# FoX bias masks behind the q and k normalisations, one weight piece loaded ahead of half of x, and x's norm begun a tick earlier

## The chip, the cores and the metric

The kernel runs on one core of one Trainium2 chip. The time is the device time of one execution in microseconds. Five engines take part: TensorE (PE, matmuls and transposes, with its weight loads listed apart as PEld), VectorE (DVE), ScalarE (ACT), GpSimd (POOL) and SyncE (SP), which issues most of the loads. Each engine works through its own instructions in the order in which they were written down. A row such as "PE ps_a L567 <- POOL raw L541" says that PE, at line 567, waited for POOL's work of line 541.

## What is computed

One decoder layer on 512 tokens of width 1024, in f32: three token mixers on the same normalised input, merged through gates, and a SwiGLU FFN. Cut to the parts that matter here:

```python
h = rms_norm(x, g_mix)
proj = h @ w_in
(q_m, k_m, v_m, q_f, k_f, v_f, f_logit, q_c, a_m, a_f, a_c) = jnp.split(proj, split_points, axis=-1)

# FoX: 8 heads of 64; cum is the running sum of the log forget gates
log_f = jax.nn.log_sigmoid(f_logit + b_forget).transpose(0, 2, 1)
q_f = rms_norm(split_heads(q_f, FOX_HEADS), g_q_fox)
k_f = rms_norm(split_heads(k_f, FOX_HEADS), g_k_fox)
scores = jnp.einsum('bhqd,bhkd->bhqk', qc, k) * scale + cq[..., None] - cum[:, :, None, :]
scores = jnp.where(causal, scores, -jnp.inf)
p = jax.nn.softmax(scores, axis=-1)

# cross attention into 256 memory tokens
mkv = rms_norm(mem, g_mem) @ w_mem_kv

merged = (sigmoid(a_m) * (y_m @ w_br_moba) + sigmoid(a_f) * (y_f @ w_br_fox)
          + sigmoid(a_c) * (y_c @ w_br_mem))
x = x + merged @ w_out
h2 = rms_norm(x, g_ffn)
x = x + (silu(h2 @ w_gate) * (h2 @ w_up)) @ w_down
```

## The kernel before

**Arithmetic.** Every f32 operand is split in two parts: ACT copies the rounded part (hi) and DVE subtracts it from the whole (lo). A product is three matmuls: hi by hi, hi by lo, lo by hi. Weights come in pieces of 128 x 1024 through SP (`load_next`, tile w_raw), and `split_next` turns each into w_hi (ACT, L223) and w_lo (DVE, L226).

**Order of the work.** All engines' orders come from one program that is written along PE's matmuls. `mm` (L291 issues the matmul) calls `tick` after each 1.25 us of matmuls by its own count, which here is every 6 matmuls of 512 columns. A tick issues at most one weight split, then what `later(n, fn)` has put off until n ticks on (`run_due`), then steps from the queue `side` (filled by `beside(steps, rate)`, so many steps a tick), and last the entries of `pend`. So a number n in `later(n, ...)` sets where an instruction stands in its engine's queue, not when it runs.

**The start.** SP loads mem in two halves, four pieces of w_mem_kv, the four tiles x0 to x3 of x (128 tokens each), then the other pieces. PE transposes mem (L436) and runs `mem_groups`, four pieces of w_mem_kv for the memory's keys, then four for its values. Beside that run the steps listed after `last_square`: squares and sums of x (`square_x`, ACT L618) and of mem (`mem_square`, ACT L451), `rsqrt` in three stages (variance: DVE L343; estimate: ACT L347 and L348; newton: DVE L351 to L353), the scaling of x (`scale_x`, L623: POOL for x0 and x1, DVE for x2 and x3), and `turn_x`, which transposes x on PE (L635). The evictions of the first memory group are ACT's raw (L519) and their squares sqh (L521).

**FoX.** The heads are done in two blocks, pairs 2 and 3 first, pairs 0 and 1 later. `head_chunk` projects q and k of a block into four quarters of raw, ACT evicts and squares them, `rsqrt` makes rr, and POOL normalises raw with rr, four instructions of 128x512 (`norm`, L541) put off by 5 to 8 ticks. With lag = 11, PE transposes the pairs 11, 13, 15 and 17 ticks on (`turn_pair`, L567), q and k in turn; ACT and DVE evict them to qT and kT (L579, L583). A tick after a k, `double` copies kT's halves across partitions, by DMAs that POOL issues (L587, L588). The forget bias of each head comes back from DRAM through ACT's queue (`load_bias`, tile ckb), and `mask_bias` writes a second copy of it with the causal mask added, one POOL instruction of 128x512 a head (L1144). `attention` runs in side steps: scores on PE (L893), bias and row minimum on DVE, exp on ACT, division on POOL (p_t, L926), transposes (L944) and values (L955) on PE. What PE does meanwhile are the gates (`gate_part`) and the branch projections (`branch_part`) of MoBA's branch.

Of the kernel before, what the change touches and what calls it, by code (L numbers as in the profile page):

```python
# [22 lines left out]
D = 1024  # L23
# [19 lines left out]
def hybrid_layer(ctx, tc, rope, x, mem, g_mix, w_in, b_forget, g_q_moba, g_k_moba, g_q_fox,  # L43
# [12 lines left out]
    def slot(name, dt=F32):  # L56
        return U.tile([P, SLOT], dt, name=name, tag="u", bufs=NSLOT)
# [3 lines left out]
    def use_table(name):  # L61
        if table[0] != name:
            act.preload_act_table_set(name)
            table[0] = name
# [16 lines left out]
    def sm(name, w, bufs=6):  # L81
        return small.tile([P, w], F32, name=name, tag=name, bufs=bufs)
# [87 lines left out]
    def load_next():  # L170
        i = loads[st["load"]]
        st["load"] += 1
        kind, src, nk, w = pieces[i]
        r = raws[i] = slot("w_raw")
        dst = r[:, :nk * w].rearrange("p (k c) -> p k c", k=nk)
        if kind == "wide":
            n = w // len(src)
            for c, part in enumerate(src):
                nc.sync.dma_start(dst[:, :, c * n:(c + 1) * n], part)
            return  # L180
        if kind == "add":
            nc.sync.dma_start(dst, src[0])
            for more in src[1:]:
                nc.gpsimd.dma_start(dst, more, accum_op=OP.add)
        else:
            nc.sync.dma_start(dst, src)
# [72 lines left out]
    pend = []  # L259
# [44 lines left out]
    def beside(steps, rate):  # L304
        side.extend((rate, fn) for fn in steps)

    def later(n, fn):
        deferred.append([n, fn])
# [18 lines left out]
    def rsqrt(ss, inv_n, w, delay=None, rows=None, nh=1, out=None):  # L327

        v, y0, a, r = (sm(i, 32, 6 if i == "rr" else 3) for i in ("rv", "ry", "ra", "rr"))
        v, y0, a = v[:, :w], y0[:, :w], a[:, :w]
        r = r[:, :w] if out is None else out

        def by_rows(o, i):
            o3, i3 = (q.rearrange("p (t h) -> p t h", h=nh) for q in (o, i))
            dve.tensor_tensor(o3, i3, rows[:, :, None].to_broadcast([P, w // nh, nh]), op=OP.mult)

        def variance():
            if rows is not None:  # L340
                by_rows(ss, ss)
                by_rows(ss, ss)
            dve.tensor_scalar(v, ss, inv_n, EPS, op0=OP.mult, op1=OP.add)  # L343

        def estimate():
            use_table("natural_log_exp_and_others")
            act.activation(a, v, AF.Ln)  # L347
            act.activation(y0, a, AF.Exp, scale=-0.5)  # L348

        def newton():  # L350
            dve.tensor_tensor(a, y0, y0, op=OP.mult)  # L351
            dve.scalar_tensor_tensor(a, a, -0.5, v, op0=OP.mult, op1=OP.mult)
            dve.scalar_tensor_tensor(r, a, 1.5, y0, op0=OP.add, op1=OP.mult)  # L353
            if rows is not None:
                by_rows(r, r)
        for n, stage in enumerate((variance, estimate, newton)):
            if delay is None:
                stage()
            else:
                later(delay + n, stage)  # L360
        return r
# [13 lines left out]
    def load_x():  # L375
        r = slot("x_t")
        t = len(x_t)
        nc.sync.dma_start(r[:, :D], x[0, t * P:(t + 1) * P, :])
        x_t.append(r)
# [11 lines left out]
    NG = 22  # L391
    GMIX, GFFN, GQF, GQM, GQC, GKF, GKM, GKC = 0, 8, 16, 17, 18, 19, 20, 21
    grow = consts.tile([NG, P], F32, name="grow")
    for _ in range(3):
        load_x()
    nc.gpsimd.dma_start(grow[0:8], g_mix.rearrange("o (k p) -> (o k) p", p=P))
    nc.gpsimd.dma_start(grow[8:16], g_ffn.rearrange("o (k p) -> (o k) p", p=P))
# [129 lines left out]
    def head_rest(raws, tw, ss, ntok, d, kind, blocks, lag, rows=None, e=2):  # L527
# [3 lines left out]
        if rows is not None:  # L531
            e = lag - 5
        rs = rsqrt(ss[:, :w], 1.0 / d, w, e, rows=rows, nh=nh)

        def of_tiles(t0, n):
# [73 lines left out]
    QF, KF_, VF = {}, {}, {}  # L609
# [5 lines left out]
    ssx = sm("ssx", NT, 1)  # L615

    def square_x(t):
        act.activation(slot("junk")[:, :D], x_t[t][:, :D], AF.Square, accum_out=ssx[:, t:t + 1])  # L618

    def scale_x(t):  # L620
        r = rsx[t // 2][:, t % 2:t % 2 + 1]
        e = pool if t < 2 else dve
        e.tensor_scalar(x_t[t][:, :D], x_t[t][:, :D], r, 1.0, op0=OP.mult, op1=OP.mult)  # L623

    rsx = {}

    def rms_x(half):
        rsx[half] = rsqrt(ssx[:, 2 * half:2 * half + 2], 1.0 / D, 2, 1)
        later(4, lambda: scale_x(2 * half))
        later(4, lambda: scale_x(2 * half + 1))  # L630

    def turn_x(k):
        tb = bank("a")
# [143 lines left out]
    def rms_mem():  # L777
        dve.tensor_reduce(ssm, ssp.rearrange("p (t a) -> p t a", a=2), axis=AX.X, op=OP.add)
        rsqrt(ssm, 1.0 / D, 2, 1, out=rs_mem)

    def both(f, *args):
        return lambda: [f(*a) for a in args]

    def last_square(t):
        square_x(t)
        rms_x(t // 2)

    beside([idle, idle, small_gains, lambda: square_x(0), lambda: last_square(1),
            lambda: square_x(2), lambda: last_square(3), both(mem_square, (0, 0), (1, 0)),
            both(mem_square, (0, 1), (1, 1)), rms_mem, idle]  # L790
           + [both(turn_x, (k,), (k + 1,)) for k in range(0, KD, 2)], 1.0)

    turn_mem(0, (split_next, split_next))
# [14 lines left out]
    YC, YM, YF = {}, {}, {}  # L808
# [275 lines left out]
    bias = {}  # L1084
# [57 lines left out]
    def mask_bias(h):  # L1142
        b = bias[h]
        pool.tensor_tensor(b[:, 512:1024].rearrange("p (a k) -> p a k", a=4),  # L1144
                           b[:, :512].rearrange("p (a k) -> p a k", a=4),
                           mz[:, None, 384:512].to_broadcast([P, 4, P]), op=OP.add)
# [4 lines left out]
    for h in (4, 5, 6, 7):  # L1151
        load_bias(h)
    for h in (4, 5, 6, 7):
        later(h, lambda h=h: mask_bias(h))
    later(17, lambda: beside(attention((2, 3), QF, KF_, VF, YF, bias), 0.7))
    for jc in (0, 1):
        gate_part(1, jc)
    for jc in (0, 1):
# [7 lines left out]
    v_chunk(VF, (0, 1))  # L1166
    for h in (0, 1, 2, 3):
        later(h + 1, lambda h=h: mask_bias(h))
    later(8, lambda: beside(attention((0, 1), QF, KF_, VF, YF, bias), 1.0))
    for jc in (2, 3):  # L1170
        gate_chunk(1, YM, jc)

# [451 lines left out]
    for p in range(NPAIR):  # L1624
# [5 lines left out]
        for m in ORDER:  # L1630
            n = at["d", m, p]
# [9 lines left out]
    for n, x in enumerate(order):  # L1641
# [3 lines left out]
        _, m, p = x  # L1645
# [49 lines left out]
```

## Time and profile before

| | us |
|---|---|
| median of 3 runs | 878.6 (877.55 to 878.94) |
| the profiled execution | 879.1 |
| its span, first to last instruction | 877.3 |
| PE busy | 849.8 (97%) |
| DVE busy | 658.1 (75%) |
| ACT busy | 471.4 (54%) |
| POOL busy | 223.1 (25%) |

The profiled execution's time is its span and 1.8 us around it. PE is busy almost throughout, and busy includes matmuls that run at the lower of the two granted clocks. A saving is therefore looked for where PE waits, and where its granted clock is below 1.

### The profile page before, as it was taken

What the parts mean: (1) busy time and instruction counts of PE and PEld (TensorE: products, weight loads), DVE (VectorE), ACT (ScalarE), POOL (GpSimd) and SP (SyncE); (2) the same over time, 40 slices, a digit from 0 to 9 for tenths busy, and PEclk for the clock granted to TensorE, in tenths of its full rate; (3) what the DMA queues carried; (4) which work ended last, traced back from release to release, by engine and by line L of the source; (5) the groups of instructions that cost most, each with busy time, mean ns of one, the idle gap of its engine ahead of it and who ended that gap; (6) DMA issues with size and microseconds to landing.
All of it is one profiled execution on the core that took longest, in us unless ns stands there. A gap on an engine that the chain in (4) does not pass through costs nothing.

```text
span 877.3 us, 13976 instructions
## 1 busy us (share of the span) xinstructions
PE 849.8 (97%) x5204; PEld 757.7 (86%) x5204; DVE 658.1 (75%) x1126; ACT 471.4 (54%) x816; POOL 223.1 (25%) x310
## 2 busy tenths in 40 slices
PE   7799999999999899999999999999999999999998
PEld 5588899799888678987888888999999999988886
DVE  4787699779677457658635845899888898997985
ACT  5855566567766546656632734544433344464671
POOL 4212218221522524244320003222311222110210
PEclk9899999999999999999999999999999999999999
DMA  9923248117521451423592536799986889775992
GB/s 310 336 30 88 57 119 216 27 49 195 129 64 41 129 121 49 121 73 85 155 240 78 172 87 144 159 193 193 179 165 124 168 169 192 174 187 146 238 249 98
DMA packets 141283, 126.10 MB, mean 144 GB/s; under 512 B 5840, under 2 KB 120072, under 8 KB 141216
## 3 DMA queue, kind: packets, MB, share of 16 engines
q1 hardware_dynamic: 107840, 95.21, 37.1%
q0 software_dynamic: 32192, 27.89, 20.8%
q10 hardware_dynamic: 1184, 2.12, 0.8%
q8 instruction: 41, 0.67, 0.3%
q14 instruction: 26, 0.21, 0.1%
HBM read 116.79 MB, written 4.21 MB: 138 GB/s over the span
## 4 chain that ended last, share of the span: by engine, by line
PE 75%; DVE 11%; ACT 6%; DMA 4%; issue 2%; POOL 2%; ACTq 0%; SPq 0%; DVEq 0%; POOLq 0%
PE ps_m L291 34%; PE ps_a L1365 12%; PE ps_m L1365 9%; PE ps_a L1518 9%; PE ps_m L1518 3%; PE ps_a L955 2%; DVE w_lo L226 2%; PE ps_a L893 2%; PE ps_a L944 2%; DMA w_raw<-in_w_mem_kv_dram 2%; ACT w_hi L223 1%; DMA kT<-kT 1%; DVE wl L1226 1%; POOL raw L541 1%; DMA mem_h<-in_mem_dram 1%
## 5 line engine op out<-in xcount | busy, mean ns | idle before, releaser
L226 DVE TENSOR_TENSOR w_lo<-w_raw,w_hi 128x1024 fp32r<-128x1024 f32 (+2 forms) x88 | 107.5, 1234 | 36.6 <-ACT w_hi L223 36.3
L291 PE MATMUL ps_m<-hT,w_hi 128*128 128x512 f32 x384 | 122.6, 401 | 0.0
L291 PE MATMUL ps_m<-w_hi,hT 128*128 128x256 f32 (+2 forms) x464 | 121.8, 337 | 0.0
L1365 PE MATMUL ps_a<-xh,wl 128*128 128x256 f32 x352 | 100.0, 284 | 1.0 <-DVE wl L1226 0.8
L1365 PE MATMUL ps_a<-xh,wh 128*128 128x256 f32 x352 | 99.8, 283 | 0.2 <-ACT wh L1223 0.2
L1365 PE MATMUL ps_a<-xl,wh 128*128 128x256 f32 x352 | 99.6, 283 | 0.0
L223 ACT ACTIVATE w_hi<-w_raw 128x1024 fp32r<-128x1024 f32 (+2 forms) x88 | 86.4, 1002 | 5.4 <-DMA w_raw<-in_w_mem_kv_dram 2.7
L291 PEld LDWEIGHTS ps_m<-w_hi,hT 128*128 128x128 f32 x464 | 80.1, 189 | 7.1
L291 PEld LDWEIGHTS ps_m<-hT,w_hi 128*128 128x128 f32 x384 | 70.9, 191 | 13.3
L1518 PE MATMUL ps_a<-dh,dr 128*128 128x512 f32 x242 | 76.6, 390 | 0.1
L291 PE MATMUL ps_m<-hT,w_lo 128*128 128x512 f32 x192 | 76.0, 396 | 0.0
L291 PE MATMUL ps_m<-w_lo,hT 128*128 128x256 f32 (+2 forms) x232 | 75.9, 327 | 0.0
L1365 PE MATMUL ps_m<-xh,wh 128*128 128x256 f32 x264 | 74.7, 283 | 0.0
L1365 PE MATMUL ps_m<-xl,wh 128*128 128x256 f32 x264 | 74.7, 283 | 0.0
L1365 PE MATMUL ps_m<-xh,wl 128*128 128x256 f32 x264 | 74.7, 283 | 0.0
L1200 POOL DMA_DIRECT2D wq<-in_w_gate_dram x22 | 32.0, 1456 | 151.7 <-DMA wq<-in_w_gate_dram 47.8
L1408 ACT ACTIVATE z<-z 128x512 f32<-128x512 f32 x22 | 13.9, 632 | 105.3 <-DVE z L741 105.3
L1365 PEld LDWEIGHTS ps_a<-xh,wl 128*128 128x128 f32 x352 | 67.5, 192 | 1.6 <-DVE wl L1226 1.6
L1226 DVE TENSOR_TENSOR wl<-wq,wh 128x1024 fp32r<-128x1024 f32 x55 | 66.9, 1218 | 2.1 <-ACT wh L1223 1.6
L1365 PEld LDWEIGHTS ps_a<-xh,wh 128*128 128x128 f32 x352 | 67.5, 192 | 0.4 <-ACT wh L1223 0.4
L1365 PEld LDWEIGHTS ps_a<-xl,wh 128*128 128x128 f32 x352 | 67.5, 192 | 0.0
L926 POOL TENSOR_SCALAR p_t<-p_t,rc 128x128 f32<-128x128 f32 (+1 forms) x64 | 36.1, 564 | 109.8 <-DVE rc L925 94.8
(271 smaller groups left out, 2212.8 us busy)
## 6 DMA issues: line engine op xcount, KB each, us to landing
w_raw<-in_w_in_dram SPq DMA_DIRECT2D x45, 512.0 KB, 4.7
wq<-in_w_gate_dram SPq DMA_DIRECT2D x55, 256.0 KB, 5.2
wq<-in_w_up_dram SPq DMA_DIRECT2D x55, 256.0 KB, 5.5
dq<-in_w_down_dram SPq DMA_DIRECT2D x25, 512.0 KB, 5.8
wq<-in_w_gate_dram POOLq DMA_DIRECT2D x22, 256.0 KB, 8.2
wq<-in_w_up_dram POOLq DMA_DIRECT2D x22, 256.0 KB, 10.4
dq<-in_w_down_dram POOLq DMA_DIRECT2D x10, 512.0 KB, 8.4
w_raw<-in_w_mem_kv_dram SPq DMA_DIRECT2D x8, 512.0 KB, 11.0
```

The source lines that it names most:

```text
L223: act.activation(hi[:, c], r[:, c], AF.Copy)
L226: dve.tensor_tensor(lo[:, c], r[:, c], f32(hi[:, c]), op=OP.subtract)
L291: pe.matmul(ps, lhsT, rhs, start=start, stop=stop)
L893: pe.matmul(ps[:, :n], Q[p][:, s * 512 + i * P:s * 512 + (i + 1) * P], K[p][s][:, b * 512:b * 512 + n], start=b == 0, stop=b == 1)
L926: pool.tensor_scalar(pt[:, :nk], pt[:, :nk], rc, 1.0, op0=OP.mult, op1=OP.mult)
L944: pe.transpose(tb[:, j * P:(j + 1) * P], pt[:, j * P:(j + 1) * P], ident)
L955: pe.matmul(yb[:, :256], V[p][:, j, 2 * s:2 * s + 2, :], PT[b][:, j, :], start=(j == 0 and b == 0), stop=(j == nj - 1 and b == 1))
L1200: e.dma_start(t[:, g * 512:(g + 1) * 512].rearrange("p (k c) -> p k c", k=4), dsrc(w, kh * 512 * DFF + f0 + fh * P, [[DFF, P], [P * DFF, 4 ...
L1226: dve.tensor_tensor(full(lo), full(r), f32(full(hi)), op=OP.subtract)
L1365: pe.matmul(ps[:, g * 256:(g + 1) * 256], w[a][:, g, k, :], r[b][:, k, :], start=n % 12 == 0, stop=n % 12 == 11)
L1408: act.activation(z[:, :, 0, :], z[:, :, 0, :], AF.Silu, scale=1.0 - 2 * j)
L1518: pe.matmul(acc_d[m][t2], r[a][:, e * 256 + t2 * P:e * 256 + (t2 + 1) * P], w[b][:, e * 512:(e + 1) * 512], start=(p == 0 and e == 0 and ( ...
```

## The change

There are three edits. In both FoX blocks the masks and the start of the attention are put off by more ticks. On SP, one more piece of weights is loaded between x1 and x2. At the start, x's squares 2 and 3 are put behind the squares of mem, and a `rsqrt` whose delay is 0 issues its variance at the end of the same tick.

```diff
         for n, stage in enumerate((variance, estimate, newton)):
             if delay is None:
                 stage()
+            elif delay + n == 0:
+                pend.append(stage)
             else:
                 later(delay + n, stage)
...
-    for _ in range(3):
+    load_x()
+    load_next()
+    for _ in range(2):
         load_x()
...
     def rms_x(half):
-        rsx[half] = rsqrt(ssx[:, 2 * half:2 * half + 2], 1.0 / D, 2, 1)
-        later(4, lambda: scale_x(2 * half))
-        later(4, lambda: scale_x(2 * half + 1))
+        rsx[half] = rsqrt(ssx[:, 2 * half:2 * half + 2], 1.0 / D, 2, 0)
+        later(2, lambda: scale_x(2 * half))
+        later(2, lambda: scale_x(2 * half + 1))
...
     beside([idle, idle, small_gains, lambda: square_x(0), lambda: last_square(1),
-            lambda: square_x(2), lambda: last_square(3), both(mem_square, (0, 0), (1, 0)),
-            both(mem_square, (0, 1), (1, 1)), rms_mem, idle]
+            both(mem_square, (0, 0), (1, 0)), both(mem_square, (0, 1), (1, 1)),
+            lambda: square_x(2), lambda: last_square(3), rms_mem, idle]
            + [both(turn_x, (k,), (k + 1,)) for k in range(0, KD, 2)], 1.0)
...
     for h in (4, 5, 6, 7):
-        later(h, lambda h=h: mask_bias(h))
-    later(17, lambda: beside(attention((2, 3), QF, KF_, VF, YF, bias), 0.7))
+        later(h + 5, lambda h=h: mask_bias(h))
+    later(19, lambda: beside(attention((2, 3), QF, KF_, VF, YF, bias), 0.7))
...
     for h in (0, 1, 2, 3):
         later(h + 1, lambda h=h: mask_bias(h))
-    later(8, lambda: beside(attention((0, 1), QF, KF_, VF, YF, bias), 1.0))
+    later(10, lambda: beside(attention((0, 1), QF, KF_, VF, YF, bias), 1.0))
```

POOL's queue at the first FoX block, before, from the first mask to the first copy of kT (ckb are the bias tiles of heads 4 to 7, raw the two tiles of q and k, rr the factor):

```order
L1144 TENSOR_TENSOR ckb_3317<-ckb_3317,mz_115 128x512
L541 TENSOR_TENSOR raw_2859<-raw_2859,rr_3316 128x512
L1144 TENSOR_TENSOR ckb_3319<-ckb_3319,mz_115 128x512
L541 TENSOR_TENSOR raw_2859<-raw_2859,rr_3316 128x512
L1144 TENSOR_TENSOR ckb_3321<-ckb_3321,mz_115 128x512
L541 TENSOR_TENSOR raw_2860<-raw_2860,rr_3316 128x512
L1144 TENSOR_TENSOR ckb_3323<-ckb_3323,mz_115 128x512
L541 TENSOR_TENSOR raw_2860<-raw_2860,rr_3316 128x512
L587 DMA kT_3480<-kT_3480 64x1024
```

The same place of POOL's queue in the changed kernel (line numbers from here on are higher by 4):

```order
L545 TENSOR_TENSOR raw_2859<-raw_2859,rr_3316 128x512 x2
L545 TENSOR_TENSOR raw_2860<-raw_2860,rr_3316 128x512 x2
L1148 TENSOR_TENSOR ckb_3317<-ckb_3317,mz_117 128x512
L1148 TENSOR_TENSOR ckb_3319<-ckb_3319,mz_117 128x512
L1148 TENSOR_TENSOR ckb_3321<-ckb_3321,mz_117 128x512
L1148 TENSOR_TENSOR ckb_3323<-ckb_3323,mz_117 128x512
L591 DMA kT_3480<-kT_3480 64x1024
```

The four normalisations now stand together ahead of the four masks; the copies of kT stay behind both.

PE's queue a little later, before, from the last transposes of this block (raw, of pair 3's k) to the first scores (kT by qT) between the matmuls of MoBA's branch projection (yT):

```order
L567 MATMUL ps_a<-ident,raw 128x128 x4
L291 MATMUL ps_m<-yT,w_hi 128x512 x2
L291 MATMUL ps_m<-yT,w_lo 128x512
L291 MATMUL ps_m<-yT,w_hi 128x512 x2
L291 MATMUL ps_m<-yT,w_lo 128x512
L893 MATMUL ps_a<-kT,qT 128x256 x2
```

And the same place of PE's queue in the changed kernel:

```order
L571 MATMUL ps_a<-ident,raw 128x128 x4
L291 MATMUL ps_m<-yT,w_hi 128x512 x2
L291 MATMUL ps_m<-yT,w_lo 128x512
L291 MATMUL ps_m<-yT,w_hi 128x512 x2
L291 MATMUL ps_m<-yT,w_lo 128x512
...
L291 MATMUL ps_m<-yT,w_hi 128x512 x2
L291 MATMUL ps_m<-yT,w_lo 128x512
L897 MATMUL ps_a<-kT,qT 128x256 x2
```

Instead of 6 matmuls, 18 stand between the last transposes and the first scores (of the 18, 9 repeat in the rows left out).

ACT's queue at the start, before, from the split of the fifth piece to that of the eighth (w_raw_154 is the fifth piece, x_t_96 and x_t_98 are x2 and x3, mem_h_74 the first half of mem, ps_m_160 and 161 the first memory group):

```order
L223 ACTIVATE w_hi_266<-w_raw_154 128x1024
L618 ACTIVATE junk_272,ssx_130<-x_t_96 128x1024
L223 ACTIVATE w_hi_281<-w_raw_200 128x1024
L347 ACTIVATE ra_258<-rv_256 128x2
L348 ACTIVATE ry_257<-ra_258 128x2
L618 ACTIVATE junk_288,ssx_130<-x_t_98 128x1024
L519 ACTIVATE raw_300<-ps_m_160 128x512
...
L223 ACTIVATE w_hi_318<-w_raw_214 128x1024
L451 ACTIVATE sqm_327,ssp_128<-mem_h_74 128x512 x2
L223 ACTIVATE w_hi_337<-w_raw_252 128x1024
```

The same stretch in the changed kernel, where w_raw_96 is the fifth piece and x_t_98 and x_t_100 are x2 and x3:

```order
L223 ACTIVATE w_hi_267<-w_raw_96 128x1024
L347 ACTIVATE ra_258<-rv_256 128x2
L348 ACTIVATE ry_257<-ra_258 128x2
L455 ACTIVATE sqm_274,ssp_130<-mem_h_74 128x512 x2
L223 ACTIVATE w_hi_284<-w_raw_200 128x1024
L455 ACTIVATE sqm_294,ssp_130<-mem_h_78 128x512 x2
L523 ACTIVATE raw_303<-ps_m_160 128x512
...
L223 ACTIVATE w_hi_321<-w_raw_214 128x1024
L622 ACTIVATE junk_326,ssx_132<-x_t_98 128x1024
L223 ACTIVATE w_hi_335<-w_raw_252 128x1024
L622 ACTIVATE junk_340,ssx_132<-x_t_100 128x1024
L223 ACTIVATE w_hi_354<-w_raw_270 128x1024
```

The squares of x2 and x3 stand behind those of mem and behind the two evictions raw (the rows left out are the first one's square sqh, the second raw and its square), one between each two of the following pieces. On DVE the Newton step of x2 and x3 now stands behind the low part of the ninth piece (w_raw_270).

## Rows read from the trace of the kernel before

**Rows 1.** What PE waited for: us in total, times, longest us.
```profile
PE ps_a L567 <- POOL raw L541: 3.8, 1, 3.8
...
PE ps_a L635 <- POOL x_t L623: 2.5, 2, 1.7
PE ps_a L635 <- DVE x_t L623: 2.0, 2, 1.8
PE ps_a L893 <- DMA kT<-kT: 1.8, 2, 1.1
...
PE ps_m L291 <- ACT raw L519: 1.2, 1, 1.2
...
PE ps_a L944 <- POOL p_t L926: 0.4, 1, 0.4
```

**Rows 2.** Timeline of PE, first FoX block: start, length, instruction, idle before.
```profile
301.26 0.49 PE L567 MATMUL ps_a<-ident,raw 128*128 128x128 f32 x3
305.52 0.48 PE L567 MATMUL ps_a<-ident,raw 128*128 128x128 f32 x1 [3.78 <-POOL raw L541]
305.65 1.20 PE L291 MATMUL ps_m<-hT,w_hi 128*128 128x512 f32 x2
...
311.33 0.70 PE L291 MATMUL ps_m<-hT,w_hi 128*128 128x512 f32 x2
...
314.52 0.71 PE L291 MATMUL ps_m<-hT,w_hi 128*128 128x512 f32 x2
...
320.06 0.47 PE L893 MATMUL ps_a<-kT,qT 128*128 128x256 f32 x2 [0.71 <-DMA kT<-kT]
```

**Rows 3.** Windows: length, busy time and instructions of each engine, granted clock, DMA.
```profile
305.60:310.90 5.30, 5.30 (x13) 4.05 (x14) 1.50 (x2) 1.36 (x2) 0.00 (x0) 0.50 0.01 3
...
36.40:41.30 4.90, 4.90 (x17) 4.22 (x18) 4.17 (x8) 1.90 (x5) 1.37 (x1) 0.50 1.07 325
```

**Rows 4.** Timeline of POOL, first FoX block.
```profile
295.73 1.04 POOL L541 TENSOR_TENSOR raw<-raw,rr 128x512 f32<-128x512 f32 x1 [3.54 <-DVE rr L353]
296.74 1.29 POOL L1144 TENSOR_TENSOR ckb<-ckb,mz 128x512 f32<-128x512 f32 x1
...
301.24 2.24 POOL L1144 TENSOR_TENSOR ckb<-ckb,mz 128x512 f32<-128x512 f32 x1
303.45 2.02 POOL L541 TENSOR_TENSOR raw<-raw,rr 128x512 f32<-128x512 f32 x1
314.25 0.57 POOL L587 DMA_DIRECT2D kT<-kT  x1 [8.78 <-DVE kT L583]
```

**Rows 5.** Timeline of DVE, first FoX block.
```profile
300.31 4.26 DVE L226 TENSOR_TENSOR w_lo<-w_raw,w_hi 128x1024 fp32r<-128x1024 f32 x2 [4.65 <-ACT w_hi L223]
```

**Rows 6.** The chain that ended last, at the first copy of kT.
```profile
314.25 5.68 DMA kT<-kT
```

**Rows 7.** Timeline of PE, second FoX block.
```profile
390.94 0.48 PE L893 MATMUL ps_a<-kT,qT 128*128 128x256 f32 x2 [1.14 <-DMA kT<-kT]
```

**Rows 8.** Timeline of ACT at the start.
```profile
17.54 1.06 ACT L618 ACTIVATE junk<-x_t 128x1024 f32<-128x1024 f32 x1 [0.57 <-DMA x_t<-in_x_dram]
...
21.43 1.06 ACT L223 ACTIVATE w_hi<-w_raw 128x1024 fp32r<-128x1024 f32 x1 [2.73 <-DMA w_raw<-in_w_mem_kv_dram]
...
25.75 0.57 ACT L519 ACTIVATE raw<-ps_m 128x512 f32<-128x512 f32 x1
...
28.04 1.04 ACT L223 ACTIVATE w_hi<-w_raw 128x1024 fp32r<-128x1024 f32 x1
28.99 0.61 ACT L451 ACTIVATE sqm<-mem_h 128x512 f32<-128x512 f32 x1
```

**Rows 9.** Timeline of DVE at the start.
```profile
33.60 0.16 DVE L353 SCALAR_TENSOR_TENSOR rr<-ra,ry 128x2 f32<-128x2 f32 x1
...
33.79 1.22 DVE L226 TENSOR_TENSOR w_lo<-w_raw,w_hi 128x1024 fp32r<-128x1024 f32 x1
34.93 1.41 DVE L623 TENSOR_SCALAR x_t<-x_t,rr 128x1024 f32<-128x1024 f32 x2
```

## The prediction

> **What bounds the kernel now.** I read the list of what TensorE (PE) waited for first, because PE is busy in nearly the whole span and only its waits and its slow clock can be won back. The list is short [rows 1]. Its longest entry is one wait of 3.8 us, at the transposes of FoX's normalised raw (L567) for GpSimd's L541. Two more entries are the transposes of x (L635), 2.5 and 2.0 us, at the start of the kernel. The FoX scores (L893) waited 1.8 us, in two waits, for the copies of kT, and 1.2 us went to ACT's raw, also at the start.
>
> Then I read PE's own timeline at the first FoX block [rows 2]. The reader is to see three things. The first transposes start at 301.26, three of the four run, and the fourth waits until 305.52. After it 12 matmuls and 4 transposes take from 305.65 to 311.33, 5.68 us, where the same 12 and 4 take 3.19 us from 311.33 to 314.52. And the first scores wait 0.71 us at 320.06. The windows view names the reason for the 5.68: the granted clock is 0.50 there, the lower level of 1.2 GHz, after PE had stood still, and again from 36.4 to 41.3 us, after the waits at x [rows 3].
>
> GpSimd's timeline says why the fourth transpose was late [rows 4]. Its queue is in order, and each normalisation of raw (L541, 1.04 us) has a mask (L1144, 1.29 us) ahead of it. The first normalisation starts at 295.73, when DVE's rr is there, the last one at 303.45; the last mask and the last normalisation take 2.24 and 2.02 us instead of 1.29 and 1.04. In the same stretch DVE needs 4.26 us for two w_lo [rows 5].
>
> **Part 1, the masks behind the normalisations (first FoX block).** No instruction is added or removed; four masks move behind four normalisations. The four then run from 295.73, one every 1.01 us (295.73 to 296.74), and end at 299.8. DVE's w_lo come at 300.31, so nothing slows these four. PE reaches the first transposes at 301.26 as before, since nothing ahead of that is touched: slack 1.4 us. So the wait of 3.78 us goes, and with it the half clock behind it, 5.68 - 3.19 = 2.49 us.
>
> What is late next? The masks now run from 299.8 beside the two w_lo. Alone they would end at 299.8 + 4 x 1.29 = 305.0. If masks and w_lo take turns, as the slow rows suggest, two w_lo of 1.22 us [rows 9] come in between and the masks end near 307.4. Behind them in GpSimd's queue stand the copies of kT (L587, L588), and the scores wait for those. The first copy was issued at 314.25 [rows 4], 2.9 us after 311.33, the first matmul behind the second group of transposes. That matmul now comes at about 301.6 + 3.19 = 304.8, so the copy is ready to go at 307.7, just after the masks even in the worse case. It took 5.68 us to land [rows 6]: 313.4.
>
> Attention starts two ticks later (17 to 19), which is 12 matmuls. PE reaches the first scores after three stretches of 3.19 us and 18 more matmuls, 4.2 to 4.8 us: at 315.4 or later, two microseconds after the landing. So the wait of 0.71 us goes too. The two ticks cost PE nothing: the 12 matmuls only change places with the scores, and the last of the attention still stands ahead of the merge that needs it. Late from where on? A copy issued after 309.7 (5.68 us ahead of 315.4) would cost its delay.
>
> By the Trainium skill, page SBUF — State Buffer, section Who interferes with whom, an elementwise operation of VectorE with both inputs in SBUF and a GpSimd instruction that reads SBUF keep each other out for a whole instruction. The trace agrees: 2.24, 2.02 and twice 2.13 us in place of 1.29, 1.04 and 1.22. By that rule the masks, gathered where the w_lo are, are what speaks against this change: they would end at 307.4 and not at 305.0, and the sum would be the same by both, with less slack by the rule.
>
> **Part 2, the second FoX block.** There the masks already stood behind the normalisations, so only the later start of attention (8 to 10) counts. The scores at 390.94 waited 1.14 us for the copy of kT [rows 7], which had therefore landed by 390.9. PE would come to them 12 matmuls, some 2.8 us, later than at 389.8, at 392.6: the whole 1.14 us goes.
>
> **Part 3, the start.** Three edits: w_mem_kv's fifth piece is loaded between x1 and x2, x's squares 2 and 3 move behind those of mem, and the variance of x is issued at once instead of a tick later. x1 landed at 17.5 (ACT's square at 17.54 waited for it) and the fifth piece at 21.4 [rows 8], with two pieces of x between: 1.3 us each. So the fifth piece now lands at 18.8, ACT's idling of 2.73 us is filled, and PE gets through the fifth and sixth pieces about a microsecond earlier. But that gain is given back, since PE then needs all four x, scaled.
>
> For x2 and x3 I add up ACT's new order from the sixth piece on, which arrives at 22.75 (a slot of 1.3 us behind 21.4, as before): w_hi 0.95, two squares of mem 1.23, two raw with their squares 2.29 (25.75 to 28.04), w_hi 0.95, square 1.04, w_hi 0.95, square 1.04 [rows 8]. That ends at 31.2. DVE then does a small one, a w_lo of 1.22, another small one, a second w_lo (its w_hi is there at 32.2), three small ones of 0.16 and the two scalings of 1.41 us [rows 9]: 31.2 + 0.3 + 2.44 + 0.5 + 1.41 and a handover or two make 36.0. Before, they ended at 34.93 + 1.41 = 36.34. PE stands idle some 6 us in one piece instead of in several and resumes 0.34 us earlier. The clock was low from there to 41.3 before [rows 3]; I expect the same again. Bounds of this part: if the low clock is over earlier, up to 2.5 us more are won (half of the 4.9); if one more w_lo of 1.22 us gets ahead of the scaling and the low clock reaches as much further, 1.9 us are lost. I take 0.34, what the rows give.
>
> The loads behind are unmoved: the queue holds the same pieces, only x2 and x3 come one slot of 1.3 us later, and their squares now start long after that.
>
> **The sum.** 3.78 + 2.49 + 0.71 + 1.14 + 0.34 = 8.46 us. A gap is counted from the modelled end of a matmul, which lies a little over 0.1 us behind the moment when the next one could have begun, so three closed gaps are worth some 0.4 us more (an estimate from a row's 0.39 us a matmul against 3.19 us for 12 with 4 transposes): 8.9 us. Against the profiled execution's 879.1 us that is 870.2. The profile is 0.5 above the median of the runs, 878.6, so the median would be 869.7; I give 870.0.
>
> **Rivals.**
> - *Part of it comes back at the kT copies or in the attention.* The masks run beside DVE and the copies behind them; if the first copy is issued at 312 instead of 307.7, the scores wait 2 us. The steps of attention also lie beside other chunks now. For it: the slow rows. Against it: 2 us of slack. Time 872 to 873.5. Chance 0.13.
> - *The start gives more.* PE idles in one piece, the clock falls earlier and is back earlier: 2.5 us more, 867.5. For it: the idling starts a microsecond earlier. Against it: in both low stretches the clock came back some 5 us after PE had resumed [rows 2, 3]. Chance 0.07.
> - *The edit doesn't do what it says:* the wait moves whole to the scores. If the copy of kT landed as late as before (issued at 314.25, landed at 319.9), PE would stand from 315.4 to 319.9 and fall to the low clock again: 4.5 + 2.5 us of the 8.9 given back, 877. It decides when something else than the transposes holds the copy, and no row shows such a thing. Chance 0.03.
> - *Slower.* Attention's units run through DVE, ACT and GpSimd, and PE waits where a p_t is late; before, this cost 0.4 us in a single wait [rows 1]. Two ticks later, 32 units of the two FoX attentions meet other evictions. At 0.4 us a unit that is 12.8 us, and 879.1 - 8.9 + 12.8 = 883. It decides from (8.9 + 1.8) / 32 = 0.33 us a unit on. Against it: the pace of units to ticks is unchanged, and the list has this wait only once. Chance 0.03.
>
> **How the numbers follow.** The forecast, 870.0, has 0.74, and its own range is 868.5 to 871.8. The range that should hold 8 in 10 takes in the rival at the copies and the larger gain at the start: 867.5 to 873.5. Within 0.2% (1.8 us, about what a measurement of this kernel can tell) begins at 876.8, and only the last two rivals reach there: faster 0.94, same 0.03, slower 0.03.
>
> **What would show it.** Right: in the changed kernel no wait of PE for L545 (the new number of L541), granted clock 1.00 from 300 to 315, no wait at either first score, masks of up to 2.2 us beside w_lo, the first kT copy issued near 307.7. At the start no wait of PE for the fifth piece, one shorter one for raw, then one long wait until about 36 and a clock of 0.50 behind it. Wrong: a wait at the scores for kT, or PE resuming behind x later than 36.4.

## The result, and the profile after

The changed kernel takes 868.73 us (median of 4, 868.44 to 869.47), the kernel before 878.77 us beside it (median of 4): ratio 0.989 with a 95% interval of 0.9873 to 0.9907, a gain of 9.7 us by the ratio (8.2 to 11.2), 10.0 by the medians. Forecast: 870.0, range 867.5 to 873.5. The profiled execution took 868.44 us, its span is 866.6 us (877.3 before), its mean granted clock 0.996 (0.992 before).

The list of what PE waited for in the changed kernel answers to [rows 1]; columns: us in total, times, longest.

```profile
PE ps_a L639 <- DVE x_t L627: 5.1, 2, 4.9
...
PE ps_m L291 <- ACT raw L523: 1.1, 1, 1.1
...
PE ps_a L948 <- POOL p_t L930: 0.4, 1, 0.4
```

No entry is left for L571 (L567 before) on POOL, and none for L897 (L893 before) on kT. What the two entries for x held is now one long wait of 4.9 us and a short one. The next three fences show the first FoX block, for [rows 2, 4, 5]: PE's, POOL's and DVE's timelines of the changed kernel (start, duration, engine and line).

```profile
300.25 0.60 PE L571 MATMUL ps_a<-ident,raw 128*128 128x128 f32 x4
300.60 0.71 PE L291 MATMUL ps_m<-hT,w_hi 128*128 128x512 f32 x2
...
314.39 0.28 PE L897 MATMUL ps_a<-kT,qT 128*128 128x256 f32 x1
```

```profile
294.04 4.05 POOL L545 TENSOR_TENSOR raw<-raw,rr 128x512 f32<-128x512 f32 x4 [15.42 <-DVE rr L353]
298.06 7.03 POOL L1148 TENSOR_TENSOR ckb<-ckb,mz 128x512 f32<-128x512 f32 x4
306.74 0.58 POOL L591 DMA_DIRECT2D kT<-kT  x1 [1.65 <-DVE kT L587]
```

```profile
290.35 1.23 DVE L226 TENSOR_TENSOR w_lo<-w_raw,w_hi 128x1024 fp32r<-128x1024 f32 x1
...
293.76 0.19 DVE L353 SCALAR_TENSOR_TENSOR rr<-ra,ry 128x32 f32<-128x32 f32 x1
299.30 4.63 DVE L226 TENSOR_TENSOR w_lo<-w_raw,w_hi 128x1024 fp32r<-128x1024 f32 x2 [5.35 <-ACT w_hi L223]
```

The four transposes run together at 300.25, the four normalisations have ended at 298.1, and the masks follow beside the w_lo. The first kT copy starts at 306.74, held by DVE's kT and not by the masks, which end at 305.1; the scores at 314.39 do not wait. Now the windows view of the changed kernel, for [rows 3] (after each engine's busy time stand the granted clock, the DMA share and GB/s).

```profile
30.00:36.00 6.00, 0.88 (x4) 0.56 (x4) 4.73 (x11) 4.55 (x10) 0.00 (x0) 0.79 1.09 349
36.00:41.00 5.00, 5.00 (x21) 4.28 (x20) 3.80 (x7) 2.09 (x5) 1.37 (x1) 0.57 1.03 324
305.00:311.00 6.00, 6.00 (x32) 4.95 (x32) 3.50 (x5) 2.98 (x5) 1.19 (x3) 1.00 0.51 113
```

In the FoX block the clock stays at 1.00; at the start the low level (1.2 GHz) remains. Last, ACT's and PE's timelines at the start, for [rows 8, 9].

```profile
18.64 1.06 ACT L223 ACTIVATE w_hi<-w_raw 128x1024 fp32r<-128x1024 f32 x1 [0.16 <-DMA w_raw<-in_w_mem_kv_dram]
28.01 1.05 ACT L622 ACTIVATE junk<-x_t 128x1024 f32<-128x1024 f32 x1
30.00 1.04 ACT L622 ACTIVATE junk<-x_t 128x1024 f32<-128x1024 f32 x1
```

```profile
29.65 0.38 PE L639 MATMUL ps_a<-ident,x_t 128*128 128x128 f32 x2
34.97 0.48 PE L639 MATMUL ps_a<-ident,x_t 128*128 128x128 f32 x1 [4.93 <-DVE x_t L627]
```

The fifth piece is there at 18.6, as worked out, and the squares of x2 and x3 stand at 28 and 30 us; PE waits 4.93 us for the scaling behind them.

### The profile page after: what moved, and what is told of

The parts are those of the page before. It is cut to its first block, busy times and chain, and to the rows that moved or that the text cites. A ratio compares the mean times of both kernels' runs of the same rounds, so it can differ in the third digit from the quotient of the medians.

```text
span 866.6 us, 13979 instructions
## 1 busy us (share of the span) xinstructions
PE 845.9 (98%) x5204; PEld 756.8 (87%) x5204; DVE 659.1 (76%) x1126; ACT 471.9 (54%) x816; POOL 226.2 (26%) x310
## 4 chain that ended last, share of the span: by engine, by line
PE 80%; DVE 10%; ACT 5%; DMA 2%; issue 1%; POOL 1%; SPq 0%; DVEq 0%; ACTq 0%; POOLq 0%
PE ps_m L291 38%; PE ps_a L1369 12%; PE ps_m L1369 9%; PE ps_a L1522 9%; PE ps_a L959 3%; PE ps_m L1522 3%; DMA w_raw<-in_w_mem_kv_dram 2%; DVE w_lo L226 2%; PE ps_a L897 2%; PE ps_a L948 2%; ACT w_hi L223 1%; DVE wl L1230 1%; DVE w_sum L212 1%; DVE qT L587 1%; DVE xl L1315 1%
## 5 line engine op out<-in xcount | busy, mean ns | idle before, releaser
L930 POOL TENSOR_SCALAR p_t<-p_t,rc 128x128 f32<-128x128 f32 (+1 forms) x64 | 39.2, 613 | 108.1 <-DVE rc L929 92.9
```

Of the source, the lines that this page charges most:

```text
L930: pool.tensor_scalar(pt[:, :nk], pt[:, :nk], rc, 1.0, op0=OP.mult, op1=OP.mult)
```

## The experiments

The theory: the stall at the transposes is POOL's queue order, the slow clock follows from the stall, the later start of the attention removes the scores' waits, and the start is worth little. The main rival: the gain comes from somewhere else, above all the later attention or the start. The masks moved in the first FoX block only; in the second they stand at `later(h + 1, ...)` in both kernels, and there only the start of the attention moved.

**Both FoX edits apart, and the start apart.** Four kernels from the one before.

Masks alone:

```diff
-        later(h, lambda h=h: mask_bias(h))
+        later(h + 5, lambda h=h: mask_bias(h))
```

> Masks of the first FoX block behind the normalisations, both attention starts left where they were. Theory A (the wait at the transposes is GpSimd's queue order, and the half clock follows from the wait): the 3.78 us at L567 go, the clock is 1.00 from 300 to 311, and the 2.49 us behind it go as well. The scores then come at about 312, and the second copy of kT, issued near 308 as in the changed kernel (307.77) and 4.2 us underway, lands at about 312: a wait of 0 to 1 us, where 0.71 was. Second block unchanged, its 1.14 us stay. Gain 6.3 to 6.7 us, 872.2 us. Theory B (the later start of the attention carries the gain): the wait moves whole to the scores, which stand until the copies have landed, with a low clock behind it: under 2 us gained, 877 us or more.

Measured: 871.47 us, ratio 0.9934 (0.9922 to 0.9946). Its list of waits has no entry for L567. The windows view shows the clock behind the transposes, PE's timeline what is left at the first scores:

```profile
305.00:311.00 6.00, 6.00 (x32) 4.98 (x31) 3.45 (x5) 2.97 (x5) 1.13 (x3) 1.00 0.54 116
```

```profile
312.14 0.48 PE L893 MATMUL ps_a<-kT,qT 128*128 128x256 f32 x2 [0.34 <-DMA kT<-kT]
```

Attention alone (17 to 19 and 8 to 10):

```diff
-    later(17, lambda: beside(attention((2, 3), QF, KF_, VF, YF, bias), 0.7))
+    later(19, lambda: beside(attention((2, 3), QF, KF_, VF, YF, bias), 0.7))
...
-    later(8, lambda: beside(attention((0, 1), QF, KF_, VF, YF, bias), 1.0))
+    later(10, lambda: beside(attention((0, 1), QF, KF_, VF, YF, bias), 1.0))
```

> Only the two later starts of the attention (17 to 19, 8 to 10), masks and start of the kernel as before. Theory A: the stall of 3.78 us at the transposes and the half clock behind it stay, the two waits at the scores (0.71 and 1.14 us) go, and perhaps the 0.4 us in a small wait near 402: gain 1.9 to 2.3 us, 876.6 us. Theory B: 6 us or more come from here, 872 us or less. Theory C (each unit of the attention costs more when it stands two ticks later): 879 us or above.

Measured: 875.19 us, ratio 0.9971 (0.9961 to 0.9981). PE's list and the windows view of this kernel:

```profile
PE ps_a L567 <- POOL raw L541: 3.8, 2, 2.9
```

```profile
305.00:311.00 6.00, 5.15 (x13) 4.09 (x14) 1.50 (x2) 1.36 (x2) 0.80 (x1) 0.50 0.01 3
```

The stall stays, and the half clock with it; no wait for kT is left. Both edits together:

> Masks and both attention starts, start of the kernel as before. Theory A: everything but the start's share; the sum of the terms of both FoX blocks is 3.78 + 2.49 + 0.71 + 1.14 and 0.3 of tails, 8.4 us: 870.3 us. If the traces' account of the two blocks holds (9.3 to 9.7 us), 869.4 us. Theory B (the normalisations come earlier only because the start moved everything by 1 us): 872 us or more, with a wait left at the transposes.

Measured: 868.79 us, ratio 0.9906 (0.9892 to 0.992), with no wait left at the transposes or for kT. And the start's three edits alone:

> Only the three edits of the start; both FoX blocks as before. By the prediction's working 0.34 us are won, 878.4 us; by the lead that PE keeps in the changed kernel's trace from 41 us on, 0.9 us, 877.8 us. Rival (the slow clock ends so much earlier that it counts): 2.5 us or more, 876.3 us or less. The stall at the transposes (3.8 us) and both waits at the scores stay in every case.

Measured: 876.95 us, ratio 0.9993 (0.9985 to 1.0002): 0.6 us, and the interval includes none. The stall (3.8 us) and the waits at the scores (1.7 us) are still in its list.

The theory's account holds in all four: by the ratios the masks gain 5.8 us, the attention 2.5, both together 8.3 (theory A: 6.3 to 6.7, 1.9 to 2.3, and 8.4). The four times lie 0.6 to 1.5 us under the expected ones; the kernel before lies lower too, with a median of 877.68 us in its 23 executions beside these four, against 878.6 in the three runs that the forecast started from. The traces also allow a sum. From one matmul ahead of both FoX blocks (the L955 that waited 0.27 us for pt, at 264.37 in the kernel before) to one behind them (the L1365 that waited 0.76 us for wl, at 549.86) PE does the same 1433 matmuls in every version:

```
kernel                 from     to       us       less than before
before                 264.37   549.86   285.49
start alone            263.24   548.36   285.12    0.37
masks alone            263.32   541.93   278.61    6.88
attention alone        264.50   547.15   282.65    2.84
masks and attention    263.50   539.26   275.76    9.73
the whole change       263.35   539.15   275.80    9.69
```

The two edits add up (6.88 + 2.84 = 9.72), and the start adds nothing here. The column "from" shows something else: the kernel with the masks alone, whose start is that of before, reaches this place as early (263.32) as the changed kernel (263.35). So the 1.0 us that the changed kernel's trace is ahead of [rows 2] before the FoX blocks is the difference of two executions and not the change.

**A shorter wait.** Before, with only the last mask behind the normalisations:

```diff
-        later(h, lambda h=h: mask_bias(h))
+        later(h + (5 if h == 7 else 0), lambda h=h: mask_bias(h))
```

> Before, with the last mask alone put behind the normalisations. GpSimd then does the last normalisation from 301.24, beside a w_lo: it ends between 302.3 and 303.3, and the wait at the transposes is 0.6 to 1.6 us in place of 3.78. Theory A (the half clock follows a long wait only): the clock stays at 1.00 in every execution, 873.0 to 874.0 us. Theory B (any wait there may bring it): the mean granted clock of some executions is 0.992 as in those of the kernel before, the others 0.996, with 2 to 2.5 us between the two, and the median lies at 874 to 876 us.

Measured: 873.81 us, ratio 0.9963 (0.995 to 0.9976). PE's list, POOL's timeline and the windows view of this kernel:

```profile
PE ps_a L567 <- POOL raw L541: 1.6, 1, 1.6
```

```profile
299.38 3.02 POOL L541 TENSOR_TENSOR raw<-raw,rr 128x512 f32<-128x512 f32 x2
302.36 2.27 POOL L1144 TENSOR_TENSOR ckb<-ckb,mz 128x512 f32<-128x512 f32 x1
```

```profile
302.00:306.00 4.00, 3.54 (x18) 2.98 (x19) 2.98 (x3) 1.77 (x3) 2.63 (x2) 1.00 0.01 4
```

The wait is 1.57 us, as the queue's order gives it, and the profiled execution has a clock of 1.00 behind it (last row). But of 12 executions 8 took 872.7 to 874.7 us with a mean clock of 0.995 to 0.998, and 4 took 876.3 to 877.5 with 0.992 to 0.994. The median is where theory A puts it, and there are two groups, as theory B says. Whether a wait of 1.6 us brings the slow stretch in those four is not shown: they have no trace, so neither the length of their wait nor the place of their low clock is known. The groups also lie 3.5 us apart by their medians, more than the 2.49 us of a whole slow stretch.

The kernel before has two groups as well. Of its 53 executions beside all the experiments (median 878.05 us, 9.3 above the changed kernel), 34 had a mean clock of 0.992 and a median of 878.5 us, the other 19 had 0.994 to 0.996 and a median of 876.7. Its profiled execution is of the first group. One trace shows a cheaper stretch at this very place: the kernel of the next experiment, with both FoX blocks as before. Its profiled execution has a mean clock of 0.994. Its list and its windows view:

```profile
PE ps_a L569 <- POOL raw L543: 3.9, 1, 3.9
```

```profile
304.00:308.00 4.00, 3.98 (x12) 3.15 (x13) 1.50 (x2) 1.37 (x2) 0.00 (x0) 0.65 0.02 4
308.00:311.00 3.00, 3.00 (x15) 2.46 (x14) 0.28 (x1) 1.97 (x3) 0.00 (x0) 0.90 0.00 0
```

The wait is as long as in [rows 2], but the clock is low for a shorter time: from the late transpose (304.02) to the next four (308.43) it is 4.4 us, where the kernel before took 5.4 (305.52 to 310.92).

**The start's edits, one by one.** The load order alone, on the kernel before:

```diff
-    for _ in range(3):
+    load_x()
+    load_next()
+    for _ in range(2):
         load_x()
```

> Before, with only the loads reordered: the fifth piece of w_mem_kv between x1 and x2. Theory A (the early piece alone is given back at x): PE passes the fifth and sixth pieces earlier and then waits longer for x, whose squares 2 and 3 keep their place; time within 1 us of before, 877 to 878. Rival (the load is what pays at the start): 2 us or more, 875.7 us or less.

Measured: 876.65 us, ratio 0.9991 (0.9982 to 1.0): 0.8 us, where the three edits together gave 0.6, and neither is clear of noise. Then the changed kernel with the squares back in their old place, the other two edits kept:

```diff
-            both(mem_square, (0, 0), (1, 0)), both(mem_square, (0, 1), (1, 1)),
-            lambda: square_x(2), lambda: last_square(3), rms_mem, idle]
+            lambda: square_x(2), lambda: last_square(3), both(mem_square, (0, 0), (1, 0)),
+            both(mem_square, (0, 1), (1, 1)), rms_mem, idle]
```

> The changed kernel, with x's squares 2 and 3 put back in front of those of mem; the early piece and the shorter norm stay. x2 and x3 have landed by 21.2 us in the changed kernel, but are squared at 28 and 30 us. Theory A (PE's wait of 4.9 us at x is the lateness of these squares): by ACT's sum with the durations of the changed kernel's trace the scalings end near 31.3, the wait is 1 to 1.5 us, 865 us, or 862.5 if the slow clock behind it goes too. Rival (ACT's backlog of w_hi takes the wait over, at the evacuations of hT): no gain, 868 to 869 us.

Measured: 863.36 us (862.97 to 863.67), ratio 0.9838 (0.9825 to 0.9851): 5.4 us faster than the changed kernel by the medians, 4.6 by the ratios. ACT's timeline of this kernel shows the squares of x2 and x3 at 19 and 23 us, PE's the short wait, the windows the clock:

```profile
19.45 1.05 ACT L622 ACTIVATE junk<-x_t 128x1024 f32<-128x1024 f32 x1
23.00 1.04 ACT L622 ACTIVATE junk<-x_t 128x1024 f32<-128x1024 f32 x1
```

```profile
29.94 0.33 PE L639 MATMUL ps_a<-ident,x_t 128*128 128x128 f32 x1 [0.68 <-DVE x_t L627]
30.60 0.76 PE L639 MATMUL ps_a<-ident,x_t 128*128 128x128 f32 x5 [0.34 <-DVE x_t L627]
```

```profile
30.00:36.00 6.00, 5.42 (x33) 4.38 (x34) 5.29 (x8) 5.97 (x13) 0.00 (x0) 1.00 1.09 350
```

The wait of 4.93 us has become 1.02, and the clock no longer falls: its mean is 1.00 in all four executions. The time is 0.9 us above the 862.5 that theory A gave for this case. Which of the two kept edits pays is told by a kernel with both FoX edits and the shorter norm alone (loads and squares as before):

```diff
-        rsx[half] = rsqrt(ssx[:, 2 * half:2 * half + 2], 1.0 / D, 2, 1)
-        later(4, lambda: scale_x(2 * half))
-        later(4, lambda: scale_x(2 * half + 1))
+        rsx[half] = rsqrt(ssx[:, 2 * half:2 * half + 2], 1.0 / D, 2, 0)
+        later(2, lambda: scale_x(2 * half))
+        later(2, lambda: scale_x(2 * half + 1))
```

> Both FoX edits as in the changed kernel; of the start's three edits only the norm of x in two steps; load order and squares as in the kernel before. Theory A (the shorter norm is what pays, and the move of the squares is what takes it away): ACT's sum from w_hi at 21.43 with the durations of before puts the scalings of x2 and x3 at 31.2 to 32.6, PE reaches x at about 31.2: a wait of 0.5 to 1.5 us, and a clock of 1.00 behind it; 863.5 to 865.3 us. Rival (the gain of 5.4 us that the squares put back in front gave needs the early piece as well): the wait at x stays at 3 us or more with a slow clock behind it, 867 us or more.

Measured: 864.17 us (863.49 to 864.4), ratio 0.9848 (0.9829 to 0.9866), against 868.79 with the FoX edits alone. DVE's and PE's timelines and the windows view of this kernel:

```profile
30.39 1.42 DVE L625 TENSOR_SCALAR x_t<-x_t,rr 128x1024 f32<-128x1024 f32 x2
```

```profile
31.20 0.33 PE L637 MATMUL ps_a<-ident,x_t 128*128 128x128 f32 x1 [0.67 <-DVE x_t L625]
31.86 0.77 PE L637 MATMUL ps_a<-ident,x_t 128*128 128x128 f32 x5 [0.34 <-DVE x_t L625]
```

```profile
36.00:41.00 5.00, 4.31 (x27) 3.37 (x26) 4.78 (x9) 4.97 (x9) 1.37 (x1) 1.00 1.11 330
```

With the FoX edits alone PE waits 4.5 us for x in all, and the granted clock from 36 to 41 us is 0.58; here it is 1.0 us and 1.00. So the shorter norm is worth 4.6 us on top of the FoX edits (5.1 by the ratios), and the move of the squares takes it back. The early piece beside it is worth 0.8 us by the medians, which the intervals do not tell from nothing.

**Both squares in one step.** The changed kernel with both squares of x2 and x3 in one step behind x1's, and the squares of mem behind them:

```diff
-            both(mem_square, (0, 0), (1, 0)), both(mem_square, (0, 1), (1, 1)),
-            lambda: square_x(2), lambda: last_square(3), rms_mem, idle]
+            lambda: (square_x(2), last_square(3)), both(mem_square, (0, 0), (1, 0)),
+            both(mem_square, (0, 1), (1, 1)), idle, rms_mem, idle]
```

> The changed kernel, with both squares of x2 and x3 in one step directly behind x1's and the squares of mem behind them. By the same sum the scalings end near 27.5, ahead of PE's first transposes of x at 29.65. Theory A: no wait at x, 863.8 us, or 861.5 if the slow clock goes too. Rival (ACT is the bound of the start): the wait moves to raw or to hT, 866 us or more.

Measured: 862.93 us (862.45 to 863.06), ratio 0.9831 (0.9818 to 0.9844), with no entry for x_t in the list of waits and a clock of 1.00:

```profile
30.00:36.00 6.00, 5.76 (x36) 4.56 (x35) 6.00 (x9) 5.72 (x10) 0.00 (x0) 1.00 1.09 349
```

That is 1.4 us above what theory A gave for this case, and the 0.4 us between it and the kernel with the squares put back (863.36) are not clear of noise. With the loads in the old order:

> As the kernel with both squares of x2 and x3 in one step (862.93 us), with the loads in the order of before. Theory A (the early piece is worth the 0.5 to 1 us that PE waits more for the fifth and sixth pieces): ACT does w_hi at 21.43, both squares to 24.9, then w_hi of the sixth piece, a microsecond later than with the early piece; 863.5 to 864.5 us. Rival (the load order matters once x is early): 866 us or more, with a slow clock at the start again.

Measured: 865.01 us (864.49 to 865.31), ratio 0.9857 (0.9835 to 0.9879), 0.5 us above what theory A gave. PE's list and the windows view of this kernel say why:

```profile
PE ps_m L291 <- DVE w_lo L226: 3.5, 2, 3.2
```

```profile
30.00:36.00 6.00, 6.00 (x29) 4.93 (x28) 5.89 (x11) 5.90 (x9) 0.15 (x1) 0.88 1.10 350
```

With both squares ahead of the sixth piece's split, PE waits 3.2 us for that piece's w_lo, and some of the low clock is back. Here the load order counts, 2.1 us by the medians (the intervals just overlap): ACT splits the sixth piece at 22.74 with the early piece and at 25.05 without it. With the squares in the order of before its worth was not clear of noise.

## Why the prediction was right

**The stall and its clock (3.78 + 2.49).** Right. The masks alone take 6.88 us out of the traces: 3.78, 2.49, 0.37 of the first scores' wait (0.71 to 0.34), and a rest of 0.24, put down to the ends of the closed gaps. One premise was not quite so, that nothing ahead of the transposes is touched. Before, the first mask (POOL, 290.89) runs beside a w_lo, in DVE's timeline of that kernel:

```profile
291.36 1.92 DVE L226 TENSOR_TENSOR w_lo<-w_raw,w_hi 128x1024 fp32r<-128x1024 f32 x1
```

With all four masks moved the same w_lo takes 1.23 us (at 290.35 in the changed kernel; 1.92 again where only the last mask is moved), and rr and the normalisations come 0.7 us earlier, besides the 1.0 us between the two executions. It made the slack larger (2.2 us and not 1.4) and changed no term. But 2.49 is the price in an execution like the profiled one; over all executions of the kernel before it is less, since about a third have a higher mean clock and take 1.8 us less. The forecast time did not suffer from it, because the 878.6 and 879.1 that it was taken from lie in the first group too.

**Masks and w_lo.** The masks took 7.03 us, where four at the 1.29 of [rows 4] take 5.16, and two w_lo took 4.63, where two at the 1.22 of [rows 9] take 2.44. They do hold each other up, and PE waits for neither. By the Trainium skill, page SBUF — State Buffer, section Who interferes with whom, a VectorE instruction with two SBUF inputs contends with a GpSimd instruction that reads SBUF, for ports that one of them locks. An estimate by that rule, with the two w_lo wholly in between, has the masks end 2.44 us later than alone; the trace has 1.9, and the measurement decides. POOL's scaling of x0 and x1 shows the same: 2.23 us in the changed kernel, at 21.60, where DVE splits nothing until 23.67, against 4.07 before, in POOL's timeline of that kernel:

```profile
29.49 4.07 POOL L623 TENSOR_SCALAR x_t<-x_t,rr 128x1024 f32<-128x1024 f32 x2 [12.48 <-ACT w_hi L223]
```

**The scores' waits (0.71 + 1.14).** Right: both gone. The attention alone takes 2.84 us out of the traces. The step that was too small is the sum: it lacked a third wait that the later start removes as well, in PE's timeline of the kernel before,

```profile
402.59 0.30 PE L944 MATMUL ps_a<-ident,p_t 128*128 128x128 f32 x1 [0.26 <-POOL pt L940]
```

and the ends of the closed gaps. 0.71 + 1.14 + 0.26 = 2.11; the rest, 0.7, is put down to those ends and a few short hold-ups between 402 and 409, and was not added up row by row. In all, the FoX blocks gave 9.7 us in the traces where 8.5 were forecast (8.12 and 0.4 for the ends); that is nearly the whole 1.3 us by which the point was too high.

**The start (0.34).** Right in size as far as the noise allows (0.6, with an interval from -0.2 to 1.3; 0.06 between the medians with and without it on top of the FoX edits), and right that the gain at the fifth piece is given back at x. (PE idled 4.93 us and not some 6, because it resumes when the first of the two scalings has ended, at 34.97, as it did before, at 35.73; and the wait for raw did not become shorter, 1.15 us against 1.16.) But the working priced the three edits as one sum and so did not see what they are: by the medians 4.6 us gained by the shorter norm, perhaps 0.8 by the load, 5.4 lost by the move of the squares. The late squares were in the working (it had ACT done with them at 31.2; the trace has 31.1). What it did not ask is when these squares could run: at 19.45 and 23.00 where they stand first, without a wait for the load, and at 28.01 and 30.00 in the changed kernel.

**Rivals.** No part came back at the copies (first copy at 306.74, scores at 314.39 without a wait), the wait did not move to the scores, and the attention's units did not become dearer (moving it alone gained 2.5 us). The start did not give 2.5 us; that the low clock there could be removed altogether was in none of the rivals.

## What to carry to other kernels

Where an engine works in order, put what the next stage waits for ahead of what is needed later, and check by its timeline that the delayed work still ends before its own reader. Price the edits of a bundle one by one, also with the others in place: here one of three undid another, and leaving it out was worth half as much again as the whole change. And compare the mean clock of the profiled execution with that of the other executions before a slow stretch behind a wait goes into a sum at its full price.

## What was not expected of the hardware

TensorE's slow stretch behind a wait of 3.8 us does not always have the same price. With the same program, 34 of 53 executions had a mean clock of 0.992, the others 0.994 to 0.996. The traces show a clock of 0.50 from 305.6 to 310.9 us behind a wait of 3.8 us, and, in the kernel with only the loads reordered, a clock of 0.65 from 304 to 308 and 0.90 from 308 to 311 behind a wait of 3.9. The kernels without a wait at the FoX transposes spread over 0.6 to 1.0 us in 4 or 5 executions each, the kernel before over 3.0 to 3.4 us in its two sets of 23 and one of 7.
